# A 16x16 unit-triangular inverse on VectorE: column by column instead of row by row

## The chip, the cores and the metric

The kernel runs on one core of a Trainium2 chip. A core has a matrix engine (TensorE, PE in the profile, with its weight loads as PEld), a vector engine (VectorE, DVE), an engine for activations (ScalarE, ACT), a programmable engine (GpSimd, POOL) and a queue engine that issues transfers (SyncE, SP). POOL and ACT issue transfers too. The metric is the device time of one execution in microseconds; the median of several runs is compared.

## The reference, cut to what matters

The program is one inference step of a hybrid backbone with one layer, for 512 latent tokens and 128 context tokens (T = 640) of 2048 channels. The layer applies an RMS norm and modulation, an input projection `w_in`, two kinds of mixing on its output, an output projection, and a SwiGLU channel mixer with 5632 hidden channels. One of the two kinds of mixing is a bidirectional RWKV-7 scan over 16 heads of 64 channels:

```python
def step(S, inp):
    r_t, w_t, k_t, v_t, a_t, b_t = inp
    sa = jnp.einsum('bhvk,bhk->bhv', S, a_t)
    S = S * w_t[:, :, None, :] + sa[..., None] * b_t[:, :, None, :] + v_t[..., None] * k_t[:, :, None, :]
    return S, jnp.einsum('bhvk,bhk->bhv', S, r_t)
```

The other is a gMLP gate over chunks of 128 tokens. The outputs are both token streams after a final norm, and the final states of the context scan.

A scan in chunks needs, for every chunk of 64 tokens, head and direction, the inverse of a matrix "identity minus a strictly triangular matrix" of 64x64. The kernel gets it from the inverses of the 16x16 blocks on its diagonal, which it then merges on TensorE to 32 and to 64.

## The kernel before, in words

The first long stage, up to about 1110 us, computes the input projection and, woven into it, everything that the scan needs beforehand. The projection has 43 column blocks of 128 channels (24 for the scan, in three kinds `r`, `v` and `k` per pair of heads, three small ones, and 16 for the gMLP). The loop over blocks takes four pieces of 512 input rows each; a piece is loaded by SP, split by ACT (L167) and DVE (L168) into two parts, and multiplied in `win`: for each half of the tokens and each 128 rows one group of three matmuls (L189, L190, L191). The counter `wide` counts these groups.

After the groups 1 and 3 of every four, `between` hands out other work from three queues. `mixA` holds the work on finished column blocks, `mixS` the substitutions, and `mixM` the merges. A queue is a list of Python generators. Each `yield c` charges c to the queue's budget, `between` adds to the budget, and the queue runs until it is used up. `mixS` gets SUBST/4 = 1.15 per call. A `yield` of a whole number stops the queue for so many groups. So the order of the program is written out by these charges; the order on each engine is then arranged by the scheduler of the framework, by its own model of readiness.

For each of the eight head pairs `take_k` computes the triangular matrices for both directions (products L650, masked on DVE at L659 and L660), stores their 16x16 diagonal blocks to memory from POOL's queue (L690) and adds `solve(p)` to `mixS`. `solve` loads the blocks back into the tile `mix` (L795) with head and position on 80 partitions and, in each partition, two directions of 16x16 elements, and pauses for WAIT = 20 groups. Then it clears the result (L797), sets its diagonal to one (L799), and runs the substitution on DVE: for each row i one product of all rows above with column i of the matrix (L803) and one reduction (L805). Two ACT copies (L809) add the transpose, POOL stores both (L812), and `merge(p)` is added to `mixM`.

`merge` loads the blocks in the layout for TensorE from POOL's queue (eight transfers, L822), pauses for HOLD = 68 groups, and for each direction alternates small TensorE products (L840, L865, L874) with additions on DVE (L853, L857) and copies on ACT. The result goes to memory from POOL (L879).

Other lines that the prediction names: L470 shifts a block's tokens on DVE, L518, L543 and L668 are small products of the `take_` functions, L571 and L575 a root and a reciprocal, L751 to L755 the normalisation of the gMLP gate, L136 a reciprocal root on POOL, and L900 the products of the modulation, which run in this stage too. After this stage come the scan itself, the output projection and the channel mixer (L1416 to L1637).

The scratch tile `mx3` holds the products of a row, up to 15 x 15 per direction; `mx2` holds the result and its transpose.

## Time and profile before

| | |
|---|---|
| median of 3 runs | 3245.55 us (3244.21 to 3252.82) |
| profiled execution, its own time | 3255.98 us |
| its span, first to last instruction | 3254.2 us |
| mean granted TensorE clock | 0.985 |
| PE busy | 3113.8 us (96%) |
| DVE busy | 2365.7 us (73%) |
| ACT busy | 1459.9 us (45%) |
| POOL busy | 1218.3 us (37%) |

Times in the profile count from the first instruction. A busy time is the sum over the instructions of an engine. PE's matmuls are pipelined and their ends are modelled, so a busy PE need not be at its peak. A row of a group names the line, the engine, the operation, the tile written and the tiles read, the shapes (partitions x elements), the count, the total busy time in us, the mean of one in ns, and behind the bar the idle time of the engine just before these instructions, with what ended it. The chain of waits is followed back from the last instruction, at each step to what released it or to the instruction before it on its engine.

### The profile page before, as it was taken

What the parts mean: (1) busy time and instruction counts of PE and PEld (TensorE: products, weight loads), DVE (VectorE), ACT (ScalarE), POOL (GpSimd) and SP (SyncE); (2) the same over time, 40 slices, a digit from 0 to 9 for tenths busy, and PEclk for the clock granted to TensorE, in tenths of its full rate; (3) what the DMA queues carried; (4) which work ended last, traced back from release to release, by engine and by line L of the source; (5) the groups of instructions that cost most, each with busy time, mean ns of one, the idle gap of its engine ahead of it and who ended that gap; (6) DMA issues with size and microseconds to landing.
All of it is one profiled execution on the core that took longest, in us unless ns stands there. A gap on an engine that the chain in (4) does not pass through costs nothing.

```text
span 3254.2 us, 72319 instructions
## 1 busy us (share of the span) xinstructions
PE 3113.8 (96%) x28216; PEld 2872.8 (88%) x28216; DVE 2365.7 (73%) x4115; ACT 1459.9 (45%) x3197; POOL 1218.3 (37%) x1065
## 2 busy tenths in 40 slices
PE   6999999999999999999999999999999999999997
PEld 3687778777777888899899999999999999999997
DVE  4548766676676677766878778777777787887788
ACT  3344444454344444345644444444444445443365
POOL 2001121211112113422356655665665645454542
PEclk9999999999999999999999999999999999999999
DMA  9666676777678588654444344344344364553453
GB/s 371 222 197 197 192 217 181 197 205 193 184 194 227 159 275 269 200 173 151 129 130 122 106 129 127 103 128 127 108 124 121 117 189 150 162 155 105 150 165 120
DMA packets 740438, 550.88 MB, mean 169 GB/s; under 512 B 141056, under 2 KB 673504, under 8 KB 731264
## 3 DMA queue, kind: packets, MB, share of 16 engines
q1 hardware_dynamic: 727136, 532.47, 54.2%
q0 software_dynamic: 10624, 13.23, 1.8%
q8 instruction: 222, 3.64, 0.5%
q14 instruction: 120, 0.98, 0.1%
q10 hardware_dynamic: 2336, 0.57, 0.1%
HBM read 437.79 MB, written 110.95 MB: 169 GB/s over the span
## 4 chain that ended last, share of the span: by engine, by line
PE 72%; DVE 10%; DMA 7%; issue 6%; POOL 3%; ACT 2%; SPq 0%; DVEq 0%; POOLq 0%; ACTq 0%
PE P L1637 15%; PE P L1635 15%; PE P L1636 15%; PE big L189 5%; PE big L191 4%; PE big L190 4%; PE pm L900 2%; DMA wt<-in_w_mod_dram 1%; DVE lo L1417 1%; PE pG L650 1%; PE big L1475 1%; PE big L1476 1%; PE big L1477 1%; PE big L1032 1%; DVE mx L803 1%
## 5 line engine op out<-in xcount | busy, mean ns | idle before, releaser
L1637 PE MATMUL P<-xo,lo 128*128 128x320 f32 x2352 | 728.0, 310 | 2.6 <-DVE lo L1417 2.5
L1635 PE MATMUL P<-xo,hi 128*128 128x320 f32 x2352 | 727.4, 309 | 0.7 <-ACT hi L1416 0.7
L1636 PE MATMUL P<-xo,hi 128*128 128x320 f32 x2352 | 727.2, 309 | 0.0
L1417 DVE TENSOR_TENSOR lo<-raw,hi 128x512 fp32r<-128x512 f32 x526 | 499.9, 954 | 178.0 <-ACT hi L1416 172.8
L1416 ACT CAST hi<-raw 128x512 fp32r<-128x512 f32 x526 | 327.0, 622 | 486.0 <-PE P L1636 384.6
L189 PE MATMUL big<-h_hi,hi 128*128 128x320 f32 x1376 | 450.9, 328 | 8.2 <-ACT hi L167 4.8
L1637 PEld LDWEIGHTS P<-xo,lo 128*128 128x128 f32 x2352 | 441.9, 188 | 4.0 <-DVE lo L1417 4.0
L1635 PEld LDWEIGHTS P<-xo,hi 128*128 128x128 f32 x2352 | 441.9, 188 | 1.0 <-ACT hi L1416 1.0
L1636 PEld LDWEIGHTS P<-xo,hi 128*128 128x128 f32 x2352 | 441.9, 188 | 0.0
L191 PE MATMUL big<-h_hi,lo 128*128 128x320 f32 x1376 | 434.2, 316 | 1.1 <-DVE lo L168 0.9
L190 PE MATMUL big<-h_lo,hi 128*128 128x320 f32 x1376 | 433.6, 315 | 0.6 <-DVE h_lo L351 0.6
L1545 POOL TENSOR_TENSOR raw<-raw 128x512 f32<-128x512 f32 x252 | 409.0, 1633 | 16.4 <-DVE lo L1417 4.9
L1637 PE MATMUL P<-xd,lo 128*128 128x320 f32 x1232 | 385.2, 313 | 18.7 <-DVE lo L1417 18.4
L1635 PE MATMUL P<-xd,hi 128*128 128x320 f32 x1232 | 383.1, 311 | 1.5 <-ACT hi L1416 0.6
L1636 PE MATMUL P<-xd,hi 128*128 128x320 f32 x1232 | 382.1, 310 | 0.0
L168 DVE TENSOR_TENSOR lo<-raw,hi 128x512 fp32r<-128x512 f32 x268 | 184.0, 689 | 204.0 <-ACT hi L167 193.6
L189 PEld LDWEIGHTS big<-h_hi,hi 128*128 128x128 f32 x1376 | 262.5, 191 | 76.2 <-issue 50.6
L1416 ACT CAST hi<-rawd 128x512 fp32r<-128x512 f32 (+1 forms) x288 | 168.8, 587 | 243.5 <-PE P L1636 206.4
L191 PEld LDWEIGHTS big<-h_hi,lo 128*128 128x128 f32 x1376 | 262.6, 191 | 10.8 <-issue 3.5
L190 PEld LDWEIGHTS big<-h_lo,hi 128*128 128x128 f32 x1376 | 263.3, 191 | 6.4 <-issue 1.7
L167 ACT CAST hi<-raw 128x512 fp32r<-128x512 f32 x268 | 165.1, 618 | 223.9 <-PE big L190 112.2
L1637 PEld LDWEIGHTS P<-xd,lo 128*128 128x128 f32 x1232 | 232.5, 189 | 25.6 <-DVE lo L1417 25.4
(403 smaller groups left out, 6109.2 us busy)
## 6 DMA issues: line engine op xcount, KB each, us to landing
wt<-in_w_mod_dram SPq DMA_DIRECT2D x96, 1024.0 KB
raw<-in_w_ffn_gate_dram SPq DMA_DIRECT2D x182, 256.0 KB
raw<-in_w_ffn_up_dram SPq DMA_DIRECT2D x182, 256.0 KB
rec<-d_S SPq DMA_DIRECT2D x80, 576.0 KB
raw<-in_w_in_dram SPq DMA_DIRECT2D x172, 256.0 KB
rawd<-in_w_ffn_down_dram SPq DMA_DIRECT2D x128, 256.0 KB
raw<-in_w_out_dram SPq DMA_DIRECT2D x96, 256.0 KB
xd<-d_os SPq DMA_DIRECT2D x66, 320.0 KB
```

The source lines that it names most:

```text
L167: S.copy(hi, raw)
L168: V.tensor_sub(lo, raw, hi.bitcast(F32))
L189: TE.matmul(halves[hf], hi[:, k, :], h_hi[:, kb, s], start=(kb == 0), stop=False)
L190: TE.matmul(halves[hf], hi[:, k, :], h_lo[:, kb, s], start=False, stop=False)
L191: TE.matmul(halves[hf], lo[:, k, :], h_hi[:, kb, s], start=False, stop=(kb == KB - 1))
L900: TE.matmul(pm[32 * j:32 * j + 2, :], cT[:, 2 * kb:2 * kb + 2], quad[:, j, :], start=(kb == 0), stop=(kb == KB - 1), tile_position=(0, 32 ...
L1416: S.copy(hi[:, 0:nk], raw[:, 0:nk])
L1417: V.tensor_sub(lo[:, 0:nk], raw[:, 0:nk], hi[:, 0:nk].bitcast(F32))
L1545: G.tensor_tensor(out=o[:, 0:nk], in0=p[:, 0:nk], in1=q[:, 0:nk], op=ALU.subtract)
L1635: TE.matmul(ps, hi[:, k, :], xk[:, 0, :], start=f, stop=False)
L1636: TE.matmul(ps, hi[:, k, :], xk[:, 1, :], start=False, stop=False)
L1637: TE.matmul(ps, lo[:, k, :], xk[:, 0, :], start=False, stop=l)
```

## The change: what it does

The substitution goes by columns of the matrix, not by rows of the result. First the first column of the matrix is copied into the first column of the result, for all rows at once. Then for each k from 1 to 14 row k of the result is finished; one product forms its multiples for all rows below it (15-k rows of k+1 elements), and one addition puts them into these rows. The sum that belongs to each element is the same. The reduction is gone. The charge per step is 0.55 in place of 0.4 + 0.004 i², for 14 steps in place of 15. The scratch tile shrinks from 225 to 64 elements per direction. The constant `NW` is not used anywhere.

```diff
+NW = 8
...
-    mx3 = bk.tile([80, 2, 225], F32, name="mx3", bufs=1)
+    mx3 = bk.tile([80, 2, 64], F32, name="mx3", bufs=1)
...
         tn = mx2[:, :, 0]
-        for i in range(1, 16):
-            tv = mx3[:, :, 0:i * i].rearrange("p d (j k) -> p d j k", k=i)
-            V.tensor_tensor(out=tv, in0=tn[:, :, 0:i, 0:i].rearrange("p d k j -> p d j k"),
-                            in1=gi[:, :, 0:i, i].unsqueeze(2).to_broadcast([80, 2, i, i]), op=ALU.mult)
-            V.tensor_reduce(out=tn[:, :, i, 0:i], in_=tv, axis=AX.X, op=ALU.add)
-            yield 0.4 + 0.004 * i * i
+        V.tensor_copy(tn[:, :, 1:16, 0], gi[:, :, 0, 1:16])
+        for k in range(1, 15):
+            m, n = 15 - k, k + 1
+            tv = mx3[:, :, 0:m * n].rearrange("p d (i j) -> p d i j", j=n)
+            V.tensor_tensor(out=tv, in0=tn[:, :, k, 0:n].unsqueeze(2).to_broadcast([80, 2, m, n]),
+                            in1=gi[:, :, k, k + 1:16].unsqueeze(3).to_broadcast([80, 2, m, n]), op=ALU.mult)
+            V.tensor_tensor(out=tn[:, :, k + 1:16, 0:n], in0=tn[:, :, k + 1:16, 0:n], in1=tv, op=ALU.add)
+            yield 0.55
```

## The prediction

> **What bounds the kernel now.** I read first the page's busy shares, to see which engine fills the span, and then the stage in which the substitution runs.

> ```profile
> span 3254.2 us, 72319 instructions
> PE 3113.8 (96%) x28216; PEld 2872.8 (88%) x28216; DVE 2365.7 (73%) x4115; ACT 1459.9 (45%) x3197; POOL 1218.3 (37%) x1065
> ```

> TensorE (PE) is busy for 96% of the span, VectorE (DVE) for 73%. A VectorE microsecond that is saved counts only where TensorE stands waiting for VectorE. The edited lines run once per head pair, eight times between 274.9 and 1047.9 us. The next view gives engine busy time (with instruction counts) for the stage from 240 to 1040 us and for the eight stretches from the first product of a substitution to its last reduction.

> ```profile
> 240.00:1040.00 800.00, 756.38 (x9059) 627.76 (x9058) 563.86 (x1093) 367.62 (x804) 142.84 (x233) 0.97 0.71 197
> 274.90:295.60 20.70, 18.83 (x133) 16.65 (x132) 20.32 (x50) 5.30 (x10) 0.00 (x0) 1.00 0.67 206
> 385.00:407.60 22.60, 20.61 (x147) 17.07 (x146) 21.84 (x47) 11.12 (x22) 0.00 (x0) 0.98 0.58 180
> 478.00:499.50 21.50, 19.72 (x378) 16.27 (x371) 17.66 (x45) 8.49 (x21) 1.00 (x1) 0.99 0.63 188
> 592.20:617.10 24.90, 22.38 (x304) 18.67 (x302) 24.16 (x52) 12.27 (x24) 0.36 (x1) 1.00 0.65 201
> 687.90:707.60 19.70, 18.05 (x378) 15.14 (x378) 18.95 (x46) 7.75 (x19) 1.01 (x1) 0.95 0.55 170
> 807.90:831.00 23.10, 20.07 (x146) 17.82 (x145) 21.50 (x51) 6.78 (x15) 2.75 (x3) 0.90 0.45 124
> 932.30:958.70 26.40, 24.11 (x167) 19.72 (x168) 24.18 (x51) 13.34 (x26) 0.00 (x0) 0.87 0.40 117
> 1023.30:1047.90 24.60, 24.60 (x463) 20.40 (x463) 20.98 (x49) 10.84 (x26) 2.34 (x3) 0.91 0.73 209
> sum 183.50, PE 168.36 PEld 141.74 DVE 169.58 ACT 75.89 POOL 7.46; mean PE 21.05 PEld 17.72 DVE 21.20 ACT 9.49 POOL 0.93
> ```

> The columns are the stretch, its length, then PE, weight loads, DVE, ACT and POOL. Over the whole stage DVE is busy 563.86 of 800 us (70%), but in the eight stretches 169.58 of 183.50 (92%): there it is full and everything behind it is late. Yet PE is idle for only 43.6 us of the 800 and 15.1 us of the 183.5. That is all the idle time the page shows to be won.

> Who made PE idle? The chain of waits that ended last, cut to each stretch, shows whether the substitution lies on it (L803 is its product, L805 its reduction), and the timeline shows each idle of PE and its releaser in brackets.

> ```profile
> by line: DVE mx L803 30.7%; DVE mx L805 19.2%; issue 13.3%; DVE zv L470 12.1%; DVE lo L168 7.0%; DVE zv L697 3.9%; DVE sp L769 3.9%; DVE gq L708 3.5%; DVE vt L755 3.5%; DVE gq L707 2.0%; DVE praw L712 0.5%; DVE praw L772 0.5%; DVEq L168 0.2
> by line: DVE mx L803 22.9%; DVE ssq L575 18.3%; DVE mx L805 15.0%; DVE zv L470 12.4%; PE pm L900 6.5%; issue 6.3%; DVE lo L168 5.6%; DVE zv L697 3.5%; DVE ssq L569 3.5%; PE pvt L543 3.3%; PE big L189 3.1%; PE big L190 0.6%; PE big L191 0.6%
> by line: DVE mx L803 15.9%; PE pm L900 11.1%; PE big L189 10.7%; DVE mx L805 9.8%; PE big L190 8.0%; PE big L191 7.3%; PE pmm L518 6.8%; PE pW L682 6.7%; issue 6.0%; DVE TB L853 4.5%; PE pblk L840 4.0%; ACT Z L684 3.9%; DVE zv L470 3.6%; DV
> by line: DVE ssq L575 16.8%; DVE zv L470 11.1%; DVE mx L803 10.0%; PE pmm L518 9.5%; DVE mx L805 9.4%; issue 6.1%; PE big L190 4.9%; DVE lo L168 4.8%; PE big L189 4.3%; PE pm L900 3.9%; PE big L191 3.5%; PE pM L865 3.3%; DVE ssq L569 3.2%;
> by line: DVE mx L803 26.4%; DVE mx L805 17.2%; DVE zv L470 8.5%; issue 7.0%; DVE TB L853 4.9%; PE pblk L840 4.4%; DVE lo L168 4.2%; ACT Z L684 4.2%; DVE gq L708 3.7%; ACT gq L710 3.7%; DVE vt L754 3.7%; DVE sp L769 3.0%; ACT hi L167 2.6%; P
> by line: PE big L189 22.0%; PE big L190 19.7%; PE big L191 19.7%; issue 13.2%; PE psp L768 7.4%; PE pmm L518 6.4%; PE ptm L175 4.7%; PE pm L900 4.2%; PE pT L874 2.9%
> by line: PE big L190 18.8%; PE big L189 18.2%; PE big L191 17.1%; DMA mix<-dd 13.2%; PE pm L900 10.7%; PE pW L682 9.6%; PE pmm L518 9.4%; issue 2.7%; PE pvt L543 2.6%; DVE zk L470 2.2%; PE pwa L592 2.2%; PE pwa L591 2.2%; DVE nkk L564 2.0%;
> by line: PE big L189 20.3%; PE big L190 17.4%; PE big L191 15.9%; PE pblk L840 11.9%; PE pW L682 8.0%; PE pm L900 7.8%; PE pT L874 7.5%; PE pmm L518 5.3%; PE psp L768 5.0%; PE pM L865 3.0%
> 303.99 2.33 PE L518 MATMUL pmm<-sqk,bones 128*128 128x320 f32 x4 [2.01 <-ACT sqk L566]
> 405.07 0.77 PE L543 MATMUL pvt<-ident,zv 128*128 128x128 f32 x5 [2.00 <-DVE zv L470]
> 494.72 0.88 PE L840 MATMUL pblk<-TB,M 32*32 32x32 f32 x80 [1.58 <-DVE TB L853]
> 611.55 0.76 PE L543 MATMUL pvt<-ident,zv 128*128 128x128 f32 x5 [1.25 <-DVE zv L470]
> 615.43 0.82 PE L865 MATMUL pM<-TB,GB 32*32 32x32 f32 x40 [1.02 <-DVE TB L853]
> 706.14 0.88 PE L840 MATMUL pblk<-TB,M 32*32 32x32 f32 x80 [1.23 <-DVE TB L853]
> ```

> The first eight rows are the stretches of the eight pairs, 0 to 7. In pairs 0 to 4 the two lines hold 49.9, 37.9, 25.7, 19.4 and 43.6% of the chain; times the lengths (20.7, 23, 22, 25 and 20 us, as the chain was cut to whole microseconds except for pair 0) that is 10.3 + 8.7 + 5.7 + 4.9 + 8.7 = 38.3 us. In pairs 5 to 7 the chain runs through PE's own matmuls, and neither line shows. But what PE itself loses behind the five chains are the six idles: 2.01 (reached through the first chain's ACT square, whose input DVE was late with), 2.00, 1.58, 1.25, 1.02 and 1.23, together **9.1 us**.

> **The change, part by part.** The durations come from these groups (count, then total and mean of one in ns, then idle before).

> ```profile
> L803 DVE TENSOR_TENSOR mx<-mx,mix 80x2 f32<-80x2 f32 (+14 forms) x120 | 53.2, 443 | 17.0 <-DMA mix<-dd 14.6
> L805 DVE TENSOR_REDUCE mx<-mx 80x2 f32<-80x2 f32 (+14 forms) x120 | 38.1, 318 | 2.1
> L803 DVE TENSOR_TENSOR mx<-mx,mix 80x450 f32<-80x450 f32 x8 | 7.5, 941 | 0.0
> L803 DVE TENSOR_TENSOR mx<-mx,mix 80x128 f32<-80x128 f32 x8 | 3.0, 379 | 0.3
> L754 DVE TENSOR_TENSOR vt<-vt,lng 128x640 f32<-128x640 f32 x7 | 5.7, 818 | 0.0
> L751 DVE TENSOR_TENSOR vt<-vt,grs 128x640 f32<-128x640 f32 x7 | 5.8, 824 | 7.5 <-POOL grs L136 7.5
> L1429 DVE TENSOR_TENSOR modc<-modc,prm 128x32 f32<-128x32 f32 x1 | 0.2, 184 | 0.0
> L805 DVE TENSOR_REDUCE mx<-mx 80x30 f32<-80x450 f32 x8 | 4.9, 610 | 0.0
> L178 DVE COPY modc<-ptm 128x16 f32<-128x16 f32 x8 | 1.1, 163 | 0.8 <-PE ptm L175 0.8
> ```

> *Removed:* 15 products and 15 reductions per pair, 53.2 + 38.1 = 91.3 us in all, **11.41 us per pair**. Their sizes are 2i² for i = 1 to 15, 2480 elements of each kind.

> *Added:* one copy of 30 elements, and for k = 1 to 14 a product and an addition of 2(15−k)(k+1) elements each: 28, 39, 48, 55, 60, 63, 64, 63, 60, 55, 48, 39, 28 and 15, doubled, 1330 of each kind, 2660 together. The old product cost (941−379)/(450−128) = 1.745 ns per element over 156 ns fixed; it reads both inputs 16 elements apart. Products whose last axis is contiguous cost less: between L1429 and L754, (818−184)/(640−32) = 1.043 ns over 151 ns. A factor repeated along the last axis, as in the new product, is no dearer (L751: 824 against 818). The new operations are contiguous in the last axis, so I take 28 × 0.151 + 2660 × 0.001043 = 4.23 + 2.77 = 7.00 us, and 0.16 for the copy (L178), **7.16 us per pair**. Rows of 2 to 15 elements 16 apart are what the trace doesn't show; at the old product's price everything would be 28 × 0.156 + 2660 × 0.001745 + 0.16 = 9.17. The saving is 4.25 us per pair by the first price and 2.24 by the second, 34 or 18 us of DVE in all. I take 34, because the new access is nearest to L754 and L751 in its last axis.

> [...]

> *Moved:* The lines' charges fall from 15 × 0.4 + 0.004 × 1240 = 10.96 to 14 × 0.55 = 7.70. Each call spends 4.6/4 = 1.15 on this queue, once per two groups of three wide matmuls, so the substitution is handed out over 13.4 groups in place of 19.1.

> ```profile
> 240.00:1040.00 800.00, 322.58 (x984) 187.09 (x983) 0.97 0.71 197
> L812 POOL DMA_DIRECT2D d<-mx x16 | 11.0, 693 | 130.9 <-ACT mx L809 130.9
> 1060.41 1.55 POOL L822 DMA_DIRECT2D TB<-d x2 [1.53 <-issue]
> 1080.06 0.83 PE pblk L840 x53
> ```

> The first row counts L189, one per group: 984 in 800 us, 0.81 us each. So what follows the substitution comes 5.7 × 0.81 = 4.6 us earlier: two ACT copies (L809), two POOL DMAs (L812), eight more (L822) and, 68 groups on, the merge. That is close to the 4.25 us by which DVE finishes sooner, so the data are about as early as their users. On POOL the L812 issue stands waiting for ACT's copy, 130.9 us in all, and behind it waits the reciprocal root (L136) for which L751 idled 7.5 us; that wait gets shorter, if anything. SP's queue isn't touched. For the last pair the final L822 issue starts at 1060.41, and the chain meets PE's merge blocks at 1080.06; a shift of 4.6 us on both sides changes nothing. All this I cost at nothing. The cover is that slack and PE's own matmuls, and if it fails each merge can stall PE as the 494.72 row shows, 1.58 us. The copy inherits the wait for the DMA into mix (14.6 us of DVE idle), which is unchanged.

> *The sum.* Of 34 us of DVE time the last three pairs' 12.8 go under PE's matmuls. In the other five each saving of 4.25 is longer than any idle behind it (2.27 at most, pair 3), so all 9.1 us could go, and no more than that. At least nothing goes: with DVE earlier, the next releaser is ACT (it released the 303.99 wait) or a weight DMA. Between 0 and 9.1 the trace doesn't decide which, and I take the middle, **−4.5 us**. The profiled execution took 3255.98 us, 1.8 outside its span, and would take 3251.5; the median of the runs shown is 10.4 lower, so the forecast is 3245.5 − 4.5 = **3241 us**.

> **The rivals.**

> 1. *Nothing reaches the end.* PE is the bound, DVE's gap is filled by waiting for ACT, and the six idles get other releasers. For it: 28.5 of PE's 43.6 idle us lie outside the eight stretches. Against it: five of the six are released by DVE. Time 3245.5.
> 2. *The whole chain share is won.* The five chains hold 38.3 us; 4.25/11.41 = 37% of that is 14.2 us. For it: PE's busy time hides pauses between matmuls, since their ends are modelled; DVE at 92% delays inputs that show as no idle. Against it: that is more than the 9.1 us of idle. Time 3231.3.
> 3. *Merges land on DVE's full stretches (slower).* A merge's two halves alternate PE blocks with DVE additions (L853). Where these stand behind substitution work, PE waits 1.58, 1.02 and 1.23, mean 1.28: three of 16 halves do so now. Earlier merges and another order could put all 16 there, 13 × 1.28 = 16.6 us more, less 4.5: +12.1, 3257.7. It decides from four extra waits on (4.5/1.28). Against it: shorter stretches leave less to collide with.
> 4. *The access is as slow as before* (short rows 16 elements apart): 18 us of DVE in place of 34, and half the gain, 2.4 us: 3243. [...]

> **How the numbers follow.** Forecast 0.40 (its own range 3236 to 3246), rival 1 0.27, rival 2 0.17, rival 3 0.10, rival 4 0.06. What a measurement here can tell from no change is about 0.3%, 9.7 us. Faster than that are most of rival 2 (0.14) and the forecast's lucky side (0.07), 0.21; slower most of rival 3 and a little of rival 1, 0.09; the remaining 0.70 is the same. The range must reach into both far cases: 3229 takes in rival 2 without its far half, 3254 stops short of rival 3's full price and leaves under 0.2 out together.

> **What would show it.** DVE's product and addition lines should sum to 54 to 58 us over eight pairs (over 70 would be rival 4), DVE's total fall by 30 to 35. The stretches should shrink from 23 to 15–18 us. The idles of PE before pvt, pblk and pM in them should be gone or under 0.5 us: if they are gone and the end hasn't moved, rival 1 holds and other releasers have grown; if L840 and L865 show more idle for DVE's TB, rival 3. A shift of more than 15 us either way, or one outside the first 1110 us, would make this reading wrong.

## The result, and the profile after

The changed kernel took 3225.66 us (median; 3220.89 to 3226.49), the kernel before 3245.1 us; the ratio is 0.9932 (95% interval 0.9914 to 0.995). Measured once more in another set of runs it was 0.9951 (0.9933 to 0.9969). The gain is 19.4 us by these medians and 16 to 22 us by the two ratios, about four times the 4.5 us that were forecast; 3225.66 lies outside the range of 3229 to 3254.

The page of the changed kernel, and its VectorE groups (count, then total busy and mean of one; line numbers are one higher than before ahead of the loop and three higher behind it: the product is L806, the addition L808, the copy L802):

```profile
span 3224.7 us, 72310 instructions
PE 3097.7 (96%) x28216; PEld 2861.5 (89%) x28216; DVE 2337.3 (72%) x4107; ACT 1460.7 (45%) x3197; POOL 1215.7 (38%) x1065
```

```profile
L808 DVE TENSOR_TENSOR mx<-mx,mx 80x56 f32<-80x56 f32 (+3 forms) x112 | 28.0, 250 | 2.2
L806 DVE TENSOR_TENSOR mx<-mx,mix 80x56 f32<-80x56 f32 (+3 forms) x112 | 28.0, 250 | 2.2
L802 DVE COPY mx<-mix 80x30 f32<-80x30 f32 x8 | 1.5, 192 | 16.7 <-DMA mix<-dd 16.7
```

The substitution takes 28.0 + 28.0 + 1.5 = 57.5 us of VectorE, where 8 x 7.16 = 57.3 had been worked out. Next, the busy shares from 240 to 1040 us, two of the eight stretches from the copy to the last addition, and their sum:

```profile
240.00:1040.00 800.00, 761.79 (x9235) 635.00 (x9235) 544.32 (x1110) 376.36 (x820) 149.28 (x245) 0.99 0.75 204
386.58:404.62 18.04, 16.79 (x108) 14.51 (x107) 17.28 (x45) 9.54 (x17) 0.00 (x0) 1.00 0.57 170
684.34:699.39 15.05, 14.79 (x323) 12.40 (x318) 14.44 (x44) 6.43 (x15) 1.01 (x1) 1.00 0.71 210
sum 137.57, PE 129.76 PEld 108.55 DVE 131.32 ACT 59.97 POOL 5.26; mean PE 16.22 PEld 13.57 DVE 16.41 ACT 7.50 POOL 0.66
```

The stretches shrank from 183.5 to 137.6 us, 17.2 us each, as expected. VectorE is as full in them as before (131.3 of 137.6). One column stands out that the prediction had quoted and passed over, the third from the end: the clock granted to TensorE. From 240 to 1040 us it is 0.99, and it was 0.97 before.

The same stage, from 211 us to the last product of the projection, with the same 10295 TensorE instructions in both kernels, first before and then after:

```profile
211.60:1110.10 898.50, 853.41 (x10295) 713.74 (x10295) 614.78 (x1181) 405.66 (x882) 159.53 (x258) 0.97 0.71 196
```

```profile
211.30:1089.10 877.80, 838.18 (x10295) 702.70 (x10295) 583.58 (x1176) 408.43 (x888) 159.59 (x259) 0.99 0.74 200
```

The stage is 20.7 us shorter. TensorE's idle time went from 45.1 to 39.6 us, 5.5 less, near the 4.5 of the forecast. The other 15.2 us left its *busy* time: the same instructions took 838 us in place of 853. What that is can be seen in the kernel before, in rows of one microsecond around the pause at 303.99, which the prediction had listed:

```profile
301.00:302.00 1.00, 0.98 (x7) 0.72 (x5) 1.00 (x3) 0.00 (x0) 0.00 (x0) 1.00 0.07 22
302.00:303.00 1.00, 0.00 (x0) 0.00 (x0) 0.96 (x2) 0.00 (x0) 0.28 (x1) 1.00 0.00 0
303.00:304.00 1.00, 0.01 (x1) 0.01 (x1) 0.16 (x1) 0.80 (x2) 1.00 (x2) 1.00 0.65 158
304.00:305.00 1.00, 1.00 (x2) 0.66 (x3) 0.53 (x1) 0.98 (x2) 1.00 (x3) 0.60 1.14 343
305.00:306.00 1.00, 1.00 (x3) 0.33 (x1) 0.66 (x2) 0.74 (x1) 1.00 (x2) 0.50 1.02 189
306.00:307.00 1.00, 1.00 (x5) 0.11 (x8) 0.49 (x1) 0.12 (x1) 0.73 (x2) 0.50 0.44 87
307.00:308.00 1.00, 1.00 (x9) 0.13 (x2) 0.35 (x1) 0.62 (x1) 0.59 (x1) 0.70 0.73 78
308.00:309.00 1.00, 1.00 (x7) 1.00 (x8) 1.00 (x1) 0.00 (x0) 0.73 (x2) 1.00 0.64 139
```

TensorE stands still for 2 us (third column 0.00 and 0.01), and then works for nearly 4 us at a granted clock of 0.50 to 0.70. The pause cost 2 us of idle time and about 1.7 us more (the sum of 1 minus the clock over four rows). I call such a stretch a dip. In rows of 4 us, summing (1 - clock) x 4 from 200 us to the last product of the projection, the kernel before lost 23.9 us in 9 dips and the changed one 6.8 us in 3. Counted only while TensorE is busy it is 22.2 and 6.7, and the difference, 15.5, is about the 15.2 us of busy time. Behind the dips of before stand pauses of 0.8 to 4.5 us; some pauses of 1.2 to 1.9 us had none.

The pauses over 1.2 us that are left in that stage after:

```profile
289.90 1.69 PE L903 MATMUL pm<-wt,cT 128*2 128x512 f32 x8 [2.36 <-DMA wt<-in_w_mod_dram]
335.44 0.71 PE L651 MATMUL pG<-R,X 64*128 64x128 f32 x8 [2.07 <-DVE GA L661]
571.04 1.33 PE L651 MATMUL pG<-R,X 64*128 64x128 f32 x16 [1.79 <-ACT zk L467]
657.55 0.48 PE L651 MATMUL pG<-R,X 64*128 64x128 f32 x2 [1.57 <-DVE X L636]
921.33 2.36 PE L519 MATMUL pmm<-sqk,bones 128*128 128x320 f32 x4 [1.96 <-DVE zv L698]
```

Before there were thirteen in that stage, of up to 4.51 us. Of the six that the prediction named, the one before pvt at 405.07 is left with 0.94 us at 403.74, and the other five are gone or under 0.9 us (the prediction had asked for under 0.5). New ones stand at other places, since the order of the instructions is another.

### The profile page after: what moved, and what is told of

It reads as the page before. It is cut to its first block, busy times and chain, and to the rows that moved or that the text cites. A ratio compares the mean times of both kernels' runs of the same rounds, so it can differ in the third digit from the quotient of the medians.

```text
span 3224.7 us, 72310 instructions
## 1 busy us (share of the span) xinstructions
PE 3097.7 (96%) x28216; PEld 2861.5 (89%) x28216; DVE 2337.3 (72%) x4107; ACT 1460.7 (45%) x3197; POOL 1215.7 (38%) x1065
## 4 chain that ended last, share of the span: by engine, by line
PE 72%; DVE 10%; DMA 8%; issue 5%; ACT 3%; POOL 2%; SPq 0%; DVEq 0%; POOLq 0%; ACTq 0%
PE P L1640 15%; PE P L1638 15%; PE P L1639 15%; PE big L190 5%; PE big L192 4%; PE big L191 4%; DVE lo L1420 2%; DMA wt<-in_w_mod_dram 2%; PE pm L903 1%; PE pG L651 1%; DMA raw<-in_w_in_dram 1%; PE big L1035 1%; PE big L1479 1%; PE big L1478 1%; PE big L1480 1%
## 5 line engine op out<-in xcount | busy, mean ns | idle before, releaser
L1420 DVE TENSOR_TENSOR lo<-raw,hi 128x512 fp32r<-128x512 f32 x526 | 512.0, 977 | 164.8 <-ACT hi L1419 160.3
L190 PE MATMUL big<-h_hi,hi 128*128 128x320 f32 x1376 | 450.4, 327 | 10.1 <-ACT hi L168 6.7
L191 PE MATMUL big<-h_lo,hi 128*128 128x320 f32 x1376 | 431.7, 314 | 0.5 <-DVE h_lo L352 0.5
L190 PEld LDWEIGHTS big<-h_hi,hi 128*128 128x128 f32 x1376 | 261.9, 190 | 79.0 <-issue 47.8
L169 DVE TENSOR_TENSOR lo<-raw,hi 128x512 fp32r<-128x512 f32 x268 | 183.3, 687 | 195.0 <-ACT hi L168 177.7
L191 PEld LDWEIGHTS big<-h_lo,hi 128*128 128x128 f32 x1376 | 261.8, 190 | 6.0 <-DVE h_lo L352 1.2
L168 ACT CAST hi<-raw 128x512 fp32r<-128x512 f32 x268 | 164.9, 619 | 223.8 <-PE big L191 115.8
L1640 PEld LDWEIGHTS P<-xd,lo 128*128 128x128 f32 x1232 | 232.4, 189 | 22.9 <-DVE lo L1420 22.7
```

What stands on the lines that cost most here:

```text
L168: S.copy(hi, raw)
L169: V.tensor_sub(lo, raw, hi.bitcast(F32))
L190: TE.matmul(halves[hf], hi[:, k, :], h_hi[:, kb, s], start=(kb == 0), stop=False)
L191: TE.matmul(halves[hf], hi[:, k, :], h_lo[:, kb, s], start=False, stop=False)
L1420: V.tensor_sub(lo[:, 0:nk], raw[:, 0:nk], hi[:, 0:nk].bitcast(F32))
L1640: TE.matmul(ps, lo[:, k, :], xk[:, 0, :], start=False, stop=l)
```

## The experiments

All ratios are against the kernel before, measured on the same chip in the same set of runs. Two theories stood at the start. **A:** the time goes by VectorE's work. **B:** the gain comes from the smaller charges, which move the merges earlier in the order.

**The change with the old charges.**

```diff
-            yield 0.55
+            yield 10.96 / 14
```

> The changed kernel with the charges of the old one: 14 steps of 10.96/14 = 0.783 in place of 0.55, so the substitution is handed out over about 19 groups as before and the merges come where they came; VectorE's work is that of the change (7.2 us per pair). Theory A (the time goes by VectorE's work: less of it in the eight stretches, fewer idles of TensorE, and with each idle gone a stretch at half clock behind it is gone) expects 3224 to 3232, most of the gain of 19 us. Theory B (the gain comes from the charges, which move what follows the substitution 4.6 us earlier in the order) expects 3241 to 3247, no gain.

Measured: 3238.88 us, ratio 0.9985 (0.9972 to 0.9998). VectorE's saving is all there, and three quarters of the gain are gone. That is neither theory's number.

**The old rows with the new charges.**

```diff
-            yield 0.4 + 0.004 * i * i
+            yield 7.7 / 15
```

> The kernel of before, rows and reductions (11.4 us of VectorE per pair), with the total charge of the change: 15 steps of 7.70/15 = 0.513. Theory A expects 3243 to 3250, as before or a little slower, since the same VectorE work is packed closer. Theory B expects 3224 to 3230, the gain of the change without its arithmetic.

Measured: 3236.62 us, 0.9973 (0.9962 to 0.9985). With no VectorE time saved at all, 7 to 9 us are won. Again between the two.

**The change with VectorE padded to its old work.**

```diff
+    mx4 = bk.tile([80, 2, 73], F32, name="mx4", bufs=1)
...
+            V.tensor_tensor(out=mx4, in0=gi[:, :, 0:5].rearrange("p d a b -> p d (a b)")[:, :, 0:73],
+                            in1=tn[:, :, k, 0:1].to_broadcast([80, 2, 73]), op=ALU.mult)
             yield 0.55
```

> The changed kernel with one more VectorE product per step, 80 partitions x 146 elements, whose result nobody uses; by the fit of the old rows it takes 0.30 us, 4.3 us per pair, so that VectorE works 11.4 us per pair as before, with the new charges. Theory A expects the gain to be given back: 3240 to 3248. Theory B expects 3224 to 3230, as the change.

Measured: 3237.69 us, 0.9972 (0.9959 to 0.9985). The added products took 33.7 us (301 ns each). About half of the gain was given back (7 to 13 of 16 to 22 us by the ratios), not all of it.

**No substitution steps at all.**

```diff
         for k in range(1, 15):
-            m, n = 15 - k, k + 1
-            tv = mx3[:, :, 0:m * n].rearrange("p d (i j) -> p d i j", j=n)
-            V.tensor_tensor(out=tv, ...)
-            V.tensor_tensor(out=tn[:, :, k + 1:16, 0:n], ...)
             yield 0.55
```

> The changed kernel without the products and additions of k = 1 to 14, with their charges kept; it leaves the substitution out but for its first column. VectorE works 0.2 us per pair in place of 7.2. Theory A, if it is proportional (19.4 us for 4.25 us per pair, 4.6 to 1), expects up to 32 us less than the change, and less than that as the idles run out: 3200 to 3220. Theory B expects 3224 to 3230.

This kernel leaves out the substitution but for its first column. Measured: 3260.2 us, 1.005 (1.0034 to 1.0066). It has 56 us less of VectorE's work than the change, and is 16 us *slower than before*. By this run theory A, taken as a statement about edits, falls. The view of who waited on TensorE up to 1117 us shows what took the place:

```profile
PE pW L683 <- ACT XT L675: 20.6, 7, 5.5
PE pm L898 <- DMA wt<-in_w_mod_dram: 7.5, 6, 1.9
```

(total us, times, longest). The first of these in the kernel before:

```profile
PE pW L682 <- ACT XT L674: 7.2, 3, 4.5
```

It has grown from 7.2 to 20.6 us (1.6 in the change). Nothing of it is VectorE's: ScalarE itself waited at L675 for a transfer out of its buffer (10.9 us) and for TensorE (3.4 us). The framework's scheduler orders every engine's instructions by its own model of their durations, and an edit that changes a duration in that model, or a charge, re-orders the stage. That was **theory C**: the order decides, and an edit lands by chance.

So the next kernels separate duration from order. Two change only what the scheduler doesn't see, the step of an operand in memory: the engines' instructions stay in the same order. (In the traces the order is the same on VectorE, ScalarE and GpSimd; TensorE's list differs in 4 to 48 of 28216 places, against up to 50 between two traces of one kernel, and in 4600 to 5000 where a charge or a pause was changed.) Two others change only the order.

**The old order, with a shorter product.** In place of the two inputs with elements 64 bytes apart, two with neighbouring elements. With these the kernel leaves out the inverse; only its time is read.

```diff
-            V.tensor_tensor(out=tv, in0=tn[:, :, 0:i, 0:i].rearrange("p d k j -> p d j k"),
-                            in1=gi[:, :, 0:i, i].unsqueeze(2)...
+            V.tensor_tensor(out=tv, in0=tn[:, :, 0:i, 0:i],
+                            in1=(gi[:, :, 0:i, i] if i == 1 else tn[:, :, i, 0:i]).unsqueeze(2)...
```

> The kernel of before, every engine's instructions in the same order and of the same shapes, but with the inputs of the row products (i from 2) read with a last axis of step 1: the rows of the result untransposed and, in place of the matrix column, the row of the result that is still zero, so the substitution computes nothing of use. Only the duration of the products should fall, by the fit from 1.745 to 1.043 ns per element, 1.7 us per pair, 14 us of VectorE in all. Theory A (the time goes by VectorE's work) expects the same share of the gain as of the work, 14/34 of 19 us: 3236. Theory C (the time goes by where each edit happens to put TensorE's pauses, by the order of the instructions) expects no change beyond what VectorE's own pauses hold: 3241 to 3245.

```profile
L803 DVE TENSOR_TENSOR mx<-mx 80x8 f32<-80x8 f32 (+6 forms) x112 | 37.7, 337 | 2.4
```

Measured: 3237.96 us, 0.9973 (0.9963 to 0.9983). With the eight first products (1.3 us) the line takes 39.0 us in place of 53.2. 14.2 us of VectorE less gave 9.1 us (8.8 by the ratio), **0.64 us per us**. That is theory A's number; theory C had expected 4 us at most.

**The changed order, with a longer product and addition.**

```diff
-    mx3 = bk.tile([80, 2, 64], F32, name="mx3", bufs=1)
+    mx3 = bk.tile([80, 2, 64, 4], F32, name="mx3", bufs=1)
...
-            tv = mx3[:, :, 0:m * n].rearrange("p d (i j) -> p d i j", j=n)
+            tv = mx3[:, :, 0:m * n, 0].rearrange("p d (i j) -> p d i j", j=n)
```

> The changed kernel with every engine's instructions in the same order, but the scratch tile of the products spread to every fourth element, so that the product writes and the addition reads 16 bytes apart. If the stride costs there what it cost in the old product, VectorE takes up to 0.7 ns more for each of 2660 elements, 1.9 us per pair, 15 us in all; if it costs nothing, this is a run of the changed kernel. Theory A expects 3225.7 + 8 = 3234 if VectorE is slower by that. Theory C expects 3226 to 3230.

Measured: 3236.22 us, 0.9969 (0.9957 to 0.998), against 0.9932 for the change in its own measurement. Both lines went from 28.0 to 36.3 us, and the time rose by 12 us by the ratios. Theory A had 8, theory C 4 at most.

**Only the order: before, with the pause ahead of the substitution cut by 6 groups.** `WAIT = 14`.

> The kernel of before with the pause ahead of each substitution cut from 20 groups to 14, so that the substitution and all that follows it come 6 groups (4.9 us) earlier in the order, about as far as the change moves the merges; no instruction is added or removed. Theory A expects no change: 3242 to 3248. Theory C expects a shift of either sign by up to 20 us, and a stage whose length is 1042 us of work plus TensorE's idle time plus the clock lost in half-rate stretches.

Measured: 3260.62 us, 1.0043 (1.0028 to 1.0058). Not one instruction was added or removed.

```profile
PE pblk L840 <- DMA TB<-d: 25.7, 3, 9.8
PE pmm L518 <- ACT Z L684: 7.1, 4, 4.0
```

Here the merges' products stand in TensorE's queue before their blocks have landed: 25.7 us in three pauses, a wait that the kernel before doesn't have. The two sides moved against each other: in the second pair the substitution starts at 405.8 us in place of 385.0, and the merge's first products stand at 439.7 in place of 463.5. The prediction had named this slack and costed a shift of both sides by the same time at nothing.

**Only the order: the change, with that pause raised by 6 groups.** `WAIT = 26`.

> The changed kernel with the pause ahead of each substitution raised from 20 groups to 26, so that what follows the substitution comes about where it came before the change; no instruction is added or removed. Theory A expects the gain to stay: 3223 to 3229. Theory C expects a shift of either sign by up to 20 us, with the same sum of work, idle time and lost clock.

Measured: 3255.53 us, 1.0029 (1.0017 to 1.0041), 25 to 31 us slower than the change by the ratios, by the order alone.

From these came **theory D**: at a fixed order VectorE's time reaches the end with some 0.65 us per us; a new order adds or takes up to 30 us. The next runs put it to the test, with the change itself beside them.

**The change again.** No edit.

> The changed kernel itself, beside the next two, so that all three stand against the same runs of before. Every theory expects its ratio from the first measurement, 0.9914 to 0.995. For theory D (at a fixed order VectorE's time reaches the end at about 0.65 us per us and the order adds or takes up to 30 us) and theory C alike, 3245 x 0.993 = 3223 to 3228 when before is at 3245.

Measured: 3228.72 us, 0.9951 (0.9933 to 0.9969).

**Scratch at every fourth element, again.** The edit shown above.

> The changed kernel in the same order with the scratch tile spread to every fourth element, which in its first run made VectorE's products and additions 72.6 us in place of 56.0, 16.6 more; run again beside the changed kernel. Theory D expects it 16.6 x 0.65 = 11 us slower than the changed kernel (8 to 14). Theory C (order alone) expects the two within 4 us.

Measured: 3238.82 us, 0.9977 (0.9967 to 0.9987), 10.1 us slower than the change beside it. Theory D had 11.

```profile
L806 DVE TENSOR_TENSOR mx<-mx,mix 80x56 f32<-80x56 f32 (+3 forms) x112 | 36.3, 324 | 2.2
L808 DVE TENSOR_TENSOR mx<-mx,mx 80x56 f32<-80x56 f32 (+3 forms) x112 | 36.2, 323 | 2.2
```

**Scratch at every second element.** The same with `[80, 2, 64, 2]`.

> The changed kernel in the same order with the scratch tile spread to every second element. If two elements in 16 bytes cost nothing, VectorE's products and additions stay at 250 ns and the time is that of the changed kernel within 3 us (theories C and D). If the stride costs in proportion, they take about 275 ns and theory D expects 3 to 5 us more than the changed kernel.

```profile
L806 DVE TENSOR_TENSOR mx<-mx,mix 80x56 f32<-80x56 f32 (+3 forms) x112 | 28.2, 252 | 2.2
L808 DVE TENSOR_TENSOR mx<-mx,mx 80x56 f32<-80x56 f32 (+3 forms) x112 | 28.1, 251 | 2.1
```

Measured: 3228.84 us, 0.9948 (0.9932 to 0.9964). The stride costs VectorE next to nothing here (252 and 251 ns against 250), and the time is the change's to 0.1 us.

**Three buffers for the masked products**, in the memory that the smaller scratch tile left free: in the tile of L659 (L660 in the changed kernel) `bufs=3` for `bufs=2`.

> The changed kernel with three buffers in place of two for the masked products of L659 (of before), which fit into what the smaller scratch tile set free: VectorE waited 23 us there for the transfer out of the buffer. The order of the instructions changes with it. Theory A expects a gain, 3215 to 3224. Theory D expects the gain of 23 x 0.65 = 15 us at most, and beside it a shift of either sign by up to 30 us from the new order: 3200 to 3255.

Measured: 3246.7 us, 1.0 (0.9989 to 1.0011). In the changed kernel VectorE waited for the transfer out of that buffer as this row shows:

```profile
DVE GR L660 <- DMA d_S<-GR: 25.3, 14, 3.5
```

With three buffers that wait is no longer among VectorE's longest, and yet the whole gain of the change is gone. Theory A's gain didn't come; theory D's range, 3200 to 3255, was too wide to be tested by this.

**Before, once more**, for a second trace.

> The kernel of before once more, for a second trace of it: the first was of an execution of 3256 us, above its median. Every theory expects 3243 to 3248. Theory D (a pause of TensorE of over a microsecond is followed by some microseconds at half clock, and these stretches are part of what a saved VectorE microsecond is worth) expects pauses at the same places as in the first trace, since the order is the same, and 15 to 24 us of lost clock up to the end of the projection, against 7 and 14 in the two traces of the changed kernel.

Measured: 3246.72 us, 0.9994 (0.9982 to 1.0007). The second trace lost 23.8 us of clock in 10 dips, the first 23.9 in 9; most of the pauses stand at the same places. (Both profiled executions of before, 3254 us of span, are about 10 us above its median; in both, what follows the projection took 2144 us against 2133 to 2136 for the change, though nothing differs there. Only the projection is compared here.)

**All operands apart:** scratch at every fourth element, and the result stored transposed.

```diff
-        tn = mx2[:, :, 0]
+        tn = mx2[:, :, 1].rearrange("p d a b -> p d b a")
...
-            S.copy(mx2[:, d, 1], tn[:, d].rearrange("p a b -> p b a"))
+            S.copy(mx2[:, d, 0], tn[:, d])
```

(The scratch tile is changed as above, and the two lines that clear the result go to the other half of `mx2`.)

> The changed kernel in the same order, with the scratch tile at every fourth element and the result stored transposed, so that the rows of the result are read and written 64 bytes apart as well; the transpose that ACT adds changes place. If the strides of several operands add up, VectorE takes 30 us more than the changed kernel, about what the kernel before took, and Theory D expects 0.6 of that, 18 us: 3247, the time of before, so that the order of the change by itself is worth nothing. If they don't add up, VectorE takes 17 us more and the time is that of the scratch tile alone, 3238. If it takes 30 us more and the time stays under 3241, part of the gain is the order's.

```profile
L808 DVE TENSOR_TENSOR mx<-mx,mx 80x56 f32<-80x56 f32 (+3 forms) x112 | 36.9, 330 | 2.2
L806 DVE TENSOR_TENSOR mx<-mx,mix 80x56 f32<-80x56 f32 (+3 forms) x112 | 36.4, 325 | 2.2
```

Measured: 3239.79 us, 0.9979 (0.9969 to 0.999). More operands with a stride cost hardly more than one here (325 and 330 ns against 324 and 323), so this is a third measurement of the same dose, not the double dose that was wanted.

**The sum.** For each trace: the start of the last product of the projection (L190 of before), TensorE's idle time from 200 us to there, the clock lost in dips, and what remains when both are taken off.

| kernel | end | idle | clock lost | remains |
|---|---|---|---|---|
| before, two traces | 1109.8, 1110.6 | 45.1, 45.4 | 23.9, 23.8 | 1040.8, 1041.4 |
| the change, two traces | 1088.8, 1092.0 | 39.6, 38.3 | 6.8, 13.7 | 1042.4, 1040.0 |
| change, scratch stride 2 | 1093.2 | 41.2 | 8.5 | 1043.5 |
| change, scratch stride 4, two traces | 1104.8, 1103.1 | 44.1, 49.3 | 20.5, 12.0 | 1040.2, 1041.8 |
| change, all operands apart | 1105.0 | 46.9 | 17.0 | 1041.1 |
| before, shorter product | 1097.7 | 42.3 | 12.0 | 1043.4 |
| old charges | 1100.4 | 39.4 | 22.2 | 1038.8 |
| rows, new charges | 1096.6 | 41.0 | 10.2 | 1045.4 |
| padded | 1099.2 | 40.4 | 15.4 | 1043.4 |
| no steps | 1117.3 | 57.9 | 15.4 | 1044.0 |
| before, pause 14 | 1122.0 | 62.4 | 27.3 | 1032.3 |
| change, pause 26 | 1112.0 | 45.8 | 25.6 | 1040.6 |
| three buffers | 1107.5 | 40.9 | 12.0 | 1054.6 |

In 14 of 16 traces the end is 1039 to 1045 us of work plus idle time plus lost clock. For "pause 14", where the longest pauses are (9.8 us), clock lost during a pause is counted twice; counted only while TensorE is busy it is 17.7, and 1042.1 remains. "Three buffers" has 12 us that neither column explains; the modulation products take longer there for as many instructions, and why is open. With three buffers, and in the second trace of the change:

```profile
L903 PE MATMUL pm<-wt,cT 128*2 128x512 f32 x472 | 81.0, 609 | 4.3 <-DMA wt<-in_w_mod_dram 4.3
```

```profile
L903 PE MATMUL pm<-wt,cT 128*2 128x512 f32 x472 | 68.3, 599 | 3.4 <-DMA wt<-in_w_mod_dram 3.3
```

**All executions.** A trace shows one execution, and both traces of before are of long ones, with a mean clock of 0.985 and 0.983. Every execution has its span and its mean granted clock on record, so the time lost to the clock, (1 - clock) x span, can be averaged over all executions of a kernel and set against the kernel before beside it. This is over the whole program, in mean us against before; the standard errors are 1 to 3 us.

| kernel (executions) | time | lost clock | the rest |
|---|---|---|---|
| the change again (10) | -16.1 | -7.7 | -8.4 |
| change, scratch stride 2 (6) | -16.8 | -10.3 | -6.5 |
| change, scratch stride 4 (12 and 12) | -10.5, -7.4 | -8.1, -7.3 | -2.4, -0.1 |
| change, all operands apart (12) | -6.7 | -7.7 | +1.1 |
| before, shorter product (12) | -9.2 | -1.1 | -8.1 |
| old charges (12) | -6.1 | +0.7 | -6.8 |
| rows, new charges (12) | -8.5 | -9.3 | +0.8 |
| padded (10) | -8.5 | -3.6 | -4.8 |
| no steps (6) | +15.1 | +5.6 | +9.5 |
| before, pause 14 (9) | +13.4 | +11.5 | +1.9 |
| change, pause 26 (9) | +7.9 | +10.0 | -2.1 |
| three buffers (12) | 0.0 | -5.6 | +5.5 |

The gain of the change is about half clock and half the rest. At a fixed order VectorE's time moves the rest and leaves the clock as it was: with stride 4 and with all operands apart the clock is the change's and the rest 4 to 10 us worse, and with the shorter product the clock is that of before and the rest 8.1 us better. The new charges with the old arithmetic win clock alone; the new arithmetic with the old charges wins none. The pause of 26 groups, an order alone, takes from the change 17.7 us of clock and 6.3 of the rest. ("Pause 14" can't be split this way, for its clock lost in long pauses; "padded", "no steps" and "three buffers" each have an order of their own, and show both parts.)

## Why the prediction was wrong, point by point

*The price of the edit* held: 57.5 us against 57.3, and the fit through two contiguous rows was the right one (the additions of 126 elements took 285 ns; the fit gives 282). Rival 4 is out.

```profile
L808 DVE TENSOR_TENSOR mx<-mx,mx 80x126 f32<-80x126 f32 x16 | 4.6, 285 | 0.4
```

VectorE's total fell by only 28.4 us for 33.8 saved, under the 30 to 35 that were expected; other lines took the rest.

*The idle time* nearly held: 5.5 and 7 us less in the two traces, against 4.5. That it is so near is partly luck, for 4.5 was the middle between two bounds, and new pauses at other places, such as the 2.36 and 2.07 us above, stand against those that went.

*The first step that failed* is the bound in the sum: "all 9.1 us could go, and no more than that". It took TensorE's idle time for all that there was to win. In this stage a pause can be followed by microseconds at half clock (0.50 from 305 to 307 us in the rows above), which count as busy time, and the sum had no term for them. Over two traces each, idle time fell by 6.3 us and lost clock by 13.6 us, 19.9 together, and the end of the projection moved by 19.8. Over all executions the clock's part is smaller, 7.7 of 16.1 us. The rest, 8.4 us, lies inside the prediction's 0 to 9.1; the clock came on top.

*The second step that failed* is "All this I cost at nothing", of the moved steps. Moving the charge re-orders the stage. The new charges alone, with the old rows and no VectorE time saved, win 7 to 9 us, all of it clock; with the old charges the change keeps about 5 us of its gain, none of it clock. Two kernels that only shift a pause by 6 groups came out 14 us slower than before, and 25 to 31 us slower than the change. The prediction's range had no room for that; it had treated the order as given.

*What VectorE's time is worth.* At the order of before 14.2 us less gave 9.1. At the order of the change 16.5 to 17.3 us more cost 8 to 11 us in three measurements, against the change as measured three times (0.9932, 0.9951, 0.9948 with stride 2): on average 0.9944 against 0.9975, 10 us. Both give 0.6 us per us. Times the 34 us of the change that would be 20 us, which is all of the 16 to 22 measured and leaves nothing for the order. The two kernels with one half of the change each say otherwise: the arithmetic alone won 5 to 6 us and the charges alone 7 to 9. Either the price falls after the first 15 us or so, or the orders of these two kernels cost something of their own; no kernel put the whole old time at the new order, and how the gain divides between VectorE's time and the order stays open.

*The rivals.* Rival 2 came nearest in size (14.2), and its sentence that PE's busy time hides something was right; what the traces show hidden there is the clock. Pauses between matmuls, which it had named, were not measured. Rival 3, merges on VectorE's full stretches, didn't happen in the change, where TensorE waited 1.6 us in all for VectorE's merge steps (L860 and L856). The mark that the prediction set, a shift of more than 15 us, did come and did say that this reading was incomplete.

## What to carry to other kernels

Read the granted clock in the same rows as the idle time: here a pause of TensorE of 2 us cost about 1.7 us more in the microseconds behind it, and that was booked as busy. Take the mean clock over many executions before giving it a price, since one order lost 6.8 us in one trace and 13.7 in another. Where a scheduler orders the instructions, an edit is two edits, a duration and an order; change an operand's step in memory (here every fourth element, 250 to 324 ns for a product) or anything else that the scheduler's model doesn't see, to measure the first alone, and shift a constant of the order without touching the work to see how far the second reaches. A gain smaller than that reach says little about the arithmetic until it has been measured at a fixed order.

## What the runs showed of the hardware

**Pauses and the clock.** The dips of before followed pauses of 0.8 to 4.5 us and lasted some 3 to 10 us at a granted clock of 0.5; the order of the change gave 6.8 us of lost clock in one execution and 13.7 in another. Over the ten executions of the change in its second measurement the time followed the mean clock, 3218 us at 0.992 and 3249 us at 0.983.

```profile
300.78:304.20 3.42, 1.41 (x10) 1.15 (x9) 2.35 (x4) 1.00 (x2) 1.48 (x3) 1.00 0.30 80
304.20:307.61 3.41, 3.41 (x12) 0.89 (x11) 1.68 (x3) 2.25 (x3) 2.73 (x5) 0.50 0.81 174
```

After, the pause of 2.07 us ahead of 335.44 was cut in two by the border of two windows, and no dip followed:

```profile
331.11:334.53 3.42, 2.26 (x90) 1.82 (x88) 1.82 (x4) 0.62 (x1) 0.00 (x0) 1.00 0.81 210
334.53:337.94 3.41, 2.50 (x21) 2.22 (x23) 2.60 (x7) 3.09 (x8) 1.12 (x3) 1.00 1.02 333
337.94:341.35 3.41, 3.41 (x91) 3.13 (x92) 1.07 (x4) 2.06 (x6) 1.11 (x3) 1.00 0.62 171
```

No kernel added a pause by itself, so these are counts over the pauses that the orders brought, and not the effect of a pause alone.

**Strides.** VectorE's product and addition took 250 ns with neighbouring elements in the scratch tile, 252 with every second and 324 with every fourth, and 325 and 330 when the result had a stride too. What sets the step of four apart from the step of two, no run shows.
